# A second merge product on 32x32 tiles, wide state maps, halved sample state and merged transfers in an RWKV-7 + gMLP step

## The chip, the cores and the metric

The kernel runs on one core of a Trainium2 chip. The metric is the device time of one execution, in microseconds (us). The kernel before takes 1367.78 us, the median of three runs (1367.05 to 1368.15). A core has a matrix engine (PE, with its weight loads shown as PEld), a vector engine (DVE), an activation engine (ACT), a general engine (POOL) and SP, which here only issues transfers (DMAs). ACT's queue issues some transfers too.

## The reference, cut to what matters

Two layers run over a prompt of 512 tokens and a sample of 8 sequences of 4 tokens, with the same weights. Layer 0 is RWKV-7 time mixing, layer 1 a chunked gMLP; a final norm follows.

```python
proj = h @ w_in                      # r, k, v, two low-rank inputs, z
xm = sh + (prev - sh) * mu           # token shift
wf = w0 + tanh(wd) @ w2              # decay, low rank
decay = exp(-exp(-softplus(-wf) - 0.5))
a = sigmoid(a0 + ad @ a2)
kk = kk / max(sqrt(sum(kk * kk)), 1e-12)
def step(S, inp):                    # per head, S is 64 x 64
    sa = einsum('bhvk,bhk->bhv', S, -kk_t)
    S = (S * w_t[:, :, None, :]
         + sa[..., None] * (kk_t * a_t)[:, :, None, :]
         + v_t[..., None] * k_t[:, :, None, :])
    return S, einsum('bhvk,bhk->bhv', S, r_t)
o = (group_norm(y) + bonus) * silu(z)
out = o @ w_out
```

There are 32 heads of 64. The outputs are the final activations of prompt and sample, the shift rows and the final states of layer 0 for both, and the sample's normalised gate values of layer 1.

## The kernel before, in words

**Tiling.** The heads are taken in 16 pairs, p = 0 to 15: head "even" on partitions 0 to 63 and head "odd" on 64 to 127 of one 128-wide block. The prompt is cut into 8 chunks of 64 tokens. Inside a chunk the recurrence is turned into matrix products: `gram` makes the products of the chunk's scaled rows (G, one 64x128 block per chunk and head), `lanes` and `merge` invert a unit lower triangle per chunk from 16x16 blocks up (`lanes` does the 16x16 ones on DVE, `merge` joins them to 32 and 64 by products on PE), and `chain` carries the 64x64 state from chunk to chunk. `sample` does the same for the 8 short sequences at once.

**The 16x16 blocks change layout through memory.** `gram` writes G to a scratch tensor du (four transfers), SP reads the diagonal 16x16 blocks of it back as lu, one block per partition (L553, four transfers of 16 partitions each). n, the factors of the normalisation, go the same way (dn at L509, ln at L512, four each). `lanes` works on lu (L626 to L662) and leaves lz. SP writes lz to the diagonal blocks of a scratch tensor dz (L666, four), whose other blocks stay zero, and reads it back as Zf with tokens on partitions (L668). `merge` transposes Zf on DVE (L680, into T), forms a first product pm (L690), copies it (P, L692), forms the second product pm2 (L698), copies two of its blocks per 32 back into Zf (L702), and does the same once more at the next size (L712 to L728).

**`chain`.** L771 forms pz from the inverse and copies it as XA (L778). L791 and L792 multiply XA by the G block and by BKT, the transposed key rows, into the state maps pm; pn (L797) gives the offsets. MB, RS and ND are read out of them on DVE (L799 to L807). Then sb (L811) and RS (L812) alternate seven times, PE and DVE, once per step over the chunks; py, pfs and ps (L821 to L854) give outputs and final state.

**`sample`.** W, 128 rows, is spread by a mask over eight sequences into We (128x512, L891), one product pst with BT (L894) gives the state's change, two DVE operations add and scale it (L895, L896), and pso (L900) transposes the result out.

**What sets the order.** A projection's products come in units of three matmuls (L257, L258, L259: each operand is split into a high and a low part); 64 units, 16 each for r, k, v and z of a pair, make a period. Everything else hangs on the dict PLAN: at unit 64 p + u of the stream the next step of `gram`, `lanes`, `merge` and so on is emitted (`steps`, `on`, `play`). PE keeps that order exactly; DVE, ACT, POOL and SP are ordered by the scheduler, which follows the emission with priorities. BANKS says which part of PSUM each product uses.

**Start and end.** Before the periods the constants, x, the shift state and the first weights are loaded, x is normalised and transposed (pth, L219), and the low-rank inputs are projected. In the last period `out_stream` joins the fill: it loads xT (L1099), the outputs of layer 0 (ofl, L1090) and multiplies them by the output weights (po).

Of the kernel before, what the change touches and what calls it, by code (L numbers as in the profile page):

```python
# [29 lines left out]

BANKS = {'pbk0': 's', 'plw0': 'y', 'pak': 'g', 'pge1': 'wa', 'pgo0': 'y', 'pge0': 'g', 'pv': 'g', 'pxt': 's'}

def _consts():
# [16 lines left out]
    c["d0"] = np.broadcast_to(d0, (128, LW))  # L50
    c["maskb"] = b[:, None] == np.arange(8)[None, :]
    c["rowm"] = np.stack([ar == 0, ar == 1, b % 2 == 0, b % 2 == 1], 1)
# [15 lines left out]
def build(tc, A, O, off):  # L68
# [5 lines left out]
    with ctx:  # L74
# [7 lines left out]
        cst = cp.tile([128, A["consts"].shape[1]], F32, name="cst")  # L82
        Q.dma_start(cst, A["consts"])

# [22 lines left out]
        nhalf = cp.tile([128, 16], F32, name="nhalf")  # L107
        G.memset(nhalf, -0.5)


# [33 lines left out]
        with tc.tile_pool(name="st", bufs=1) as st:  # L144
# [11 lines left out]
            load_x(0)  # L156
            load_x(1)
            Q.dma_start(r0, rows(A["norm_g"]))
            load_x(2)
# [27 lines left out]
            def stats(h):  # L187

                n = 3 - h
                ms = st.tile([128, 3], F32, name=f"ms{h}")  # L190
                if h == 0:
                    G.memset(ms, 1.0)
                    S.activation(sqj[0:32], xs, AF.Square, scale=D**-0.5, accum_out=ms[0:32, 2:3])
                S.activation(sqj, xt[:, 2 * h, :], AF.Square, scale=D**-0.5, accum_out=ms[:, 0:1])
                bs0 = st.tile([128, 2, 6], F32, name=f"bs0{h}")
                mv0 = st.tile([128, 2], F32, name=f"mv0{h}")
                for j in range(2):
                    V.bn_stats(bs0[:, j, :], xt[:, 2 * h + 1, 512 * j : 512 * j + 512])
                V.bn_aggr(mv0, bs0)
                V.tensor_scalar(ms[:, 1:2], mv0[:, 0:1], mv0[:, 0:1], mv0[:, 1:2], op0=ALU.mult, op1=ALU.add)  # L200
                G.tensor_scalar(ms[:, 0:n], ms[:, 0:n], NORM_EPS, None, op0=ALU.add)
                G.tensor_tensor(out=ms[:, 0:n], in0=ms[:, 0:n], in1=nhalf[:, 0:n], op=ALU.pow)
                return ms
# [137 lines left out]

        du = [drm.tile([4, 2, 2, 64, 64], F32, name=f"du{i}") for i in range(2)]
        dz = [drm.tile([4, 2, 2, 64, 64], F32, name=f"dz{i}") for i in range(2)]
        zz = l0.tile([128, NCH, 64], F32, name="zz", tag="Zf", bufs=2)
        G.memset(zz, 0.0)
        for x in dz:
            Q.dma_start(x.rearrange("q h a s t -> (a s) (q h) t"), zz)
        cnt = [0]
# [146 lines left out]
        def norms(p, smp=None):  # L495
# [11 lines left out]
            dn = drm.tile([4, 2, 2, 64], F32, name=f"dn{p}", tag="dn", bufs=2)  # L507
            for g in range(4):
                Q.dma_start(dn[g], n2[32 * g : 32 * g + 2].rearrange("h (a t) -> h a t", t=64))  # L509
            ln = z["ln"] = l0.tile([64, 16], F32, name=f"ln{p}", tag="ln", bufs=2)  # L510
            for i in range(4):
                Q.dma_start(ln[16 * i : 16 * i + 16], dn.rearrange("q h a t -> (q h a) t")[:, 16 * i : 16 * i + 16])  # L512

# [16 lines left out]
        def gram(p):  # L530

            z = Z[p]
            AR, BK = z["AR"], z["BK"]
            GS = z["GS"] = [l0.tile([128, NCH, 128], F32, name=f"G{n}{p}", tag="G", bufs=4) for n in "EO"]
            for q in range(2):
# [11 lines left out]
            for h in range(2):  # L547
                for a, rs in enumerate(rw_):
                    Q.dma_start(d[:, h, a].rearrange("q s t -> s q t"), GS[h][rs, a::2, 0:64])
            lu = z["lu"] = l0.tile([64, 16, 16], F32, name=f"lu{p}", tag="lu", bufs=1)  # L550
            for i in range(4):
                b = slice(16 * i, 16 * i + 16)
                Q.dma_start(lu[b], d.rearrange("q h a s t -> (q h a) s t")[:, b, b])  # L553
            yield
# [37 lines left out]
        def turn(p):  # L592

            z = Z[p]
            AR, BK, GS, v = z["AR"], z["BK"], z["GS"], xv
            BKT = z["BKT"] = l0.tile([128, NCH, 128], F32, name=f"BKT{p}", tag="BKT", bufs=1)
            for q in range(2):
                ps = wh(f"pbk{q}")
                for j in range(4):
                    T.transpose(ps[:, 128 * j : 128 * j + 128], BK[:, 4 * q + j].rearrange("p a b -> p (a b)"), ident)  # L600
                S.activation(BKT[:, 4 * q : 4 * q + 4, :], c128(ps), AF.Copy)
                yield
# [16 lines left out]
        def lanes(p):  # L619
# [43 lines left out]
            d = dz[p % 2]  # L663
            for i in range(4):
                b = slice(16 * i, 16 * i + 16)
                Q.dma_start(d.rearrange("q h a s t -> (q h a) s t")[:, b, b], lz[b])  # L666
            Zf = z["Zf"] = l0.tile([128, NCH, 64], F32, name=f"Zf{p}", tag="Zf", bufs=2)
            Q.dma_start(Zf, d.rearrange("q h a s t -> (a s) (q h) t"))  # L668

        def merge(p):  # L670
# [25 lines left out]
            for c in range(NCH):  # L696
                for rs in (e_, o_):
                    T.matmul(ps[rs, 64 * c : 64 * c + 64], P1[rs, 64 * c : 64 * c + 64], Zf[rs, c, :], start=True, stop=True)  # L698
            pz = ps.rearrange("p (c j) -> p c j", j=64)
# [56 lines left out]
        def chain(p):  # L756

            z = Z[p]
            GS, AR, W, ZR, BKT, Dt = (z[n] for n in ("GS", "AR", "W", "ZR", "BKT", "D"))
            XA = l0.tile([128, NCH, 64], F32, name=f"XA{p}", tag="XN", bufs=1)  # L760
# [24 lines left out]
            for j in range(4):  # L785
                for h, hs in enumerate(rw_):
                    for a, rs in enumerate(rw_):
                        c = 2 * j + a
                        if c:
                            x = XA[rs, 2 * j + h, :]  # L790
                            T.matmul(pa[a][hs, 128 * j : 128 * j + 64], x, GS[h][rs, c, 64:128], start=True, stop=True)  # L791
                            T.matmul(pa[a][hs, 128 * j + 64 : 128 * j + 128], x, BKT[rs, c, 64 * h : 64 * h + 64], start=True, stop=True)  # L792

            pn = bank("pn", "s")
            for c in range(NCH):
                for h, hs in enumerate(rw_):
                    T.matmul(pn[hs, 64 * c : 64 * c + 64], BKT[:, c, 64 * h : 64 * h + 64], W[:, c, 64 * h : 64 * h + 64], start=True, stop=True)  # L797
            ND = l0.tile([128, NCH, 64], F32, name=f"ND{p}", tag="XN", bufs=1)
# [35 lines left out]
        def sample(p):  # L834
# [6 lines left out]
            def w5(name):  # L841
                return lt.tile([128, 512], F32, name=f"{name}{p}", tag="m", bufs=2)

# [44 lines left out]
            V.tensor_tensor(out=ysr, in0=ps[:, 0:64], in1=GR, op=ALU.add)  # L888
            We = w5("We")
# [4 lines left out]
            T.matmul(ps, BT, We, start=True, stop=True)  # L894
            V.tensor_tensor(out=s0, in0=ps, in1=s0, op=ALU.add)  # L895
            V.tensor_tensor(out=v8(s0), in0=v8(s0), in1=z["D"][:, 8:16, None].to_broadcast([128, 8, 64]), op=ALU.mult)  # L896
# [99 lines left out]
        def finish(i):  # L996
# [4 lines left out]
        PLAN = dict(  # L1001
            gram=(38, 42, 43),
            bonus=(53, 55),
            lanes=(53, 54, 55, 57, 59, 65, 66, 67, 67, 68, 68, 70, 70, 75, 75, 75),
            lora=(62, 65, 69, 71, 74),
            fold=(55, 66, 79, 87),
            smp0=78,
            merge=(88, 92, 100, 106),
            burst=96,
            flip=91,  # L1010
            chain=(107, 117, 121, 129, 132, 135, 137, 141, 142, 142),
            smp=(107, 109, 111, 116, 119, 124),
            tail=145,
            tail_end=(151, 160),
        )
        agenda = {}

        def on(p, u, f):
            agenda.setdefault(64 * p + u, []).append(f)

# [72 lines left out]
        def out_stream():  # L1093
# [3 lines left out]
            wts = halves(*raw.pop(0))  # L1097
            for m in range(0, KD, 2):
                OQ.dma_start(xT[:, m : m + 2], xfd[:, m : m + 2])  # L1099
# [367 lines left out]
```

## Time and profile before

| what | value |
|---|---|
| median of three runs | 1367.78 us (1367.05 to 1368.15) |
| the profiled execution's own time | 1372.8 us |
| its span, mean granted clock | 1371.0 us, 0.989 |
| PE busy | 1307.7 us (95%), 14764 records |
| DVE, ACT, POOL busy | 994.0 (73%), 683.4 (50%), 163.2 (12%) us |
| gMLP part (930 to 1371) | 441.0 us, PE 433.9 busy |

The span is shorter than the execution's time by 1.8 us that lie around it. A busy PE is not PE at its peak, and a wait counts only on the chain of work that ended last; an engine's idle time elsewhere costs nothing. In the rows, "pm" stands for several products of `merge` and `chain`, which the line tells apart.

### The profile page before, as it was taken

How to read it: one execution, taken by the hardware profiler on the slowest of the kernel's cores; microseconds unless marked ns; L12 is line 12 of the kernel's file. 1: busy time of each engine (PE TensorE's matmuls, PEld its weight loads, DVE VectorE, ACT ScalarE, POOL GpSimd, SP SyncE). 2: the span in 40 equal slices, each digit the busy share in tenths (PEclk: the TensorE clock that was granted, in tenths of full speed). 3: DMA queues.
4: the chain of work that ended last, by engine and by line, in shares of the span. 5: the costliest groups of instructions: out<-in, count | busy, mean ns of one | idle time of the engine just before them, and what ended most of it. 6: DMA issues, size and time to landing. Idle time of an engine off the chain costs nothing.

```text
span 1371.0 us, 36002 instructions
## 1 busy us (share of the span) xinstructions
PE 1307.7 (95%) x14764; PEld 1228.4 (90%) x14764; DVE 994.0 (73%) x2296; ACT 683.4 (50%) x1582; POOL 163.2 (12%) x352
## 2 busy tenths in 40 slices
PE   5879999999999999999999979999999999999998
PEld 4879889888988988898898868999999999999997
DVE  5668988988898897889889767555446755656566
ACT  5555666566556656655665634234333323223334
POOL 2310222122022112102211200000000000000000
PEclk9999999999999999999999989999999999999999
DMA  4423343333333334332332254523222323232411
GB/s 149 115 64 83 85 102 90 75 105 86 93 86 98 87 76 101 78 91 68 81 82 66 69 162 129 151 66 100 77 79 80 88 72 95 66 108 60 144 54 66
DMA packets 282759, 124.30 MB, mean 91 GB/s; under 512 B 117618, under 2 KB 275460, under 8 KB 282596
## 3 DMA queue, kind: packets, MB, share of 16 engines
q1 hardware_dynamic: 262948, 106.94, 29.7%
q10 hardware_dynamic: 19648, 15.08, 3.7%
q8 instruction: 116, 1.90, 0.6%
q14 instruction: 47, 0.39, 0.1%
HBM read 102.02 MB, written 19.95 MB: 89 GB/s over the span
## 4 chain that ended last, share of the span: by engine, by line
PE 53%; DVE 23%; issue 7%; DMA 6%; ACT 5%; POOL 3%; SPq 2%; DVEq 0%; ACTq 0%; POOLq 0%
POOL m L930 3%; PE gz_p L257 3%; PE gz_p L259 2%; PE gu_p L257 2%; PE gz_p L258 2%; PE gu_p L259 2%; PE gu_p L258 2%; PE gv_p L258 2%; PE gv_p L259 2%; PE gv_p L257 2%; PE v_p L257 2%; DMA lu<-du 2%; PE go__p L258 2%; PE go__p L257 2%; PE go__p L259 2%
## 5 line engine op out<-in xcount | busy, mean ns | idle before, releaser
L257 PE MATMUL v_p<-hh,v_h 128*128 128x272 f32 x256 | 84.8, 331 | 0.0
L257 PE MATMUL k_p<-hh,k_h 128*128 128x272 f32 x256 | 81.5, 318 | 0.0
L257 PE MATMUL r_p<-hh,r_h 128*128 128x272 f32 x256 | 79.2, 309 | 0.0
L257 PE MATMUL z_p<-hh,z_h 128*128 128x272 f32 x256 | 78.2, 305 | 0.0
L257 PE MATMUL gv_p<-hh,gv_h 128*128 128x272 f32 x256 | 75.6, 295 | 0.0
L257 PE MATMUL gz_p<-hh,gz_h 128*128 128x272 f32 x256 | 75.6, 295 | 0.0
L259 PE MATMUL k_p<-hh,k_l 128*128 128x272 f32 x256 | 74.4, 291 | 1.0 <-DVE k_l L127 1.0
L259 PE MATMUL z_p<-hh,z_l 128*128 128x272 f32 x256 | 74.4, 291 | 0.0
L258 PE MATMUL z_p<-hl,z_h 128*128 128x272 f32 x256 | 74.3, 290 | 0.0
L258 PE MATMUL gv_p<-hl,gv_h 128*128 128x272 f32 x256 | 74.3, 290 | 0.0
L259 PE MATMUL gv_p<-hh,gv_l 128*128 128x272 f32 x256 | 74.2, 290 | 0.0
L257 PE MATMUL gu_p<-hh,gu_h 128*128 128x272 f32 x256 | 74.2, 290 | 0.0
L259 PE MATMUL r_p<-hh,r_l 128*128 128x272 f32 x256 | 74.0, 289 | 0.0
L258 PE MATMUL k_p<-hl,k_h 128*128 128x272 f32 x256 | 74.0, 289 | 0.0
L259 PE MATMUL gu_p<-hh,gu_l 128*128 128x272 f32 x256 | 74.0, 289 | 0.0
L258 PE MATMUL gu_p<-hl,gu_h 128*128 128x272 f32 x256 | 74.0, 289 | 0.0
L259 PE MATMUL gz_p<-hh,gz_l 128*128 128x272 f32 x256 | 74.0, 289 | 0.0
L258 PE MATMUL v_p<-hl,v_h 128*128 128x272 f32 x256 | 74.0, 289 | 0.0
L259 PE MATMUL v_p<-hh,v_l 128*128 128x272 f32 x256 | 73.9, 289 | 0.0
L258 PE MATMUL r_p<-hl,r_h 128*128 128x272 f32 x256 | 73.8, 288 | 0.0
L258 PE MATMUL gz_p<-hl,gz_h 128*128 128x272 f32 x256 | 73.8, 288 | 0.0
L378 POOL COPY shl<-raw 128x9 f32<-128x9 f32 x49 | 20.7, 423 | 292.9 <-ACT raw L375 292.9
(453 smaller groups left out, 4928.7 us busy)
## 6 DMA issues: line engine op xcount, KB each, us to landing
k_r<-rw_in SPq DMA_DIRECT2D x16, 512.0 KB
r_r<-rw_in SPq DMA_DIRECT2D x16, 512.0 KB
v_r<-rw_in SPq DMA_DIRECT2D x16, 512.0 KB
z_r<-rw_in SPq DMA_DIRECT2D x16, 512.0 KB
gv_r<-gm_in SPq DMA_DIRECT2D x16, 512.0 KB
gu_r<-gm_in SPq DMA_DIRECT2D x16, 512.0 KB
gz_r<-gm_in SPq DMA_DIRECT2D x16, 512.0 KB
go_r<-gm_out SPq DMA_DIRECT2D x24, 256.0 KB
```

Source lines behind the costliest of these rows:

```text
L257: T.matmul(ps, whi, ahi, start=first, stop=False)
L258: T.matmul(ps, whi, alo, start=False, stop=False)
L259: T.matmul(ps, wlo, ahi, start=False, stop=last)
L378: G.tensor_copy(shl[:, :, f], raw[:, 512:553:5])
L930: G.tensor_tensor(out=m2, in0=m2, in1=nhalf[:, 0:9], op=ALU.pow)
```

## The change

1. **pm2** (second product of `merge`): of each 64x64 block only the two 32x32 blocks on the diagonal are read, so only those are computed, four 32x32 products a chunk in place of two 64x64.
2. **GK**: G and BKT come to lie side by side in one tile [128, 8, 2, 192], so that one product of 128 columns replaces two of 64 for the state maps. The tile has two buffers; before G had four half-size ones, BKT one.
3. **Sample state**: the mask is taken modulo four, We has 256 columns, and two products of 256 columns, one on each half of the rows, go to two banks; two DVE additions of half width follow.
4. **Transfers**: du and dz have 65 rows a block, so that the diagonal is one regular pattern: lu and dz are one transfer each in place of four, ln one in place of four, dn two in place of four, lr (low-rank weights) two in place of four with a repeated source and one buffer in place of two. Zf becomes two, the zeroing of dz four in place of two.
5. **Start**: the constants are loaded behind xs and the first two x loads, an activation on a column of ones stands early, one small addition moves from POOL to DVE.
6. **End**: the four xT loads are spread over the first output groups.
7. **PLAN and BANKS** have other numbers. `early` with late=0 changes nothing.

```diff
@@ second product of merge
             for c in range(NCH):
-                for rs in (e_, o_):
-                    T.matmul(ps[rs, 64 * c : 64 * c + 64], P1[rs, 64 * c : 64 * c + 64], Zf[rs, c, :], start=True, stop=True)
+                for b0 in range(4):
+                    rs, j0 = slice(32 * b0, 32 * b0 + 32), 32 * (b0 % 2)
+                    js = slice(64 * c + j0, 64 * c + j0 + 32)
+                    T.matmul(ps[rs, js], P1[rs, js], Zf[rs, c, j0 : j0 + 32], start=True, stop=True)
@@ wide operand
-            GS = z["GS"] = [l0.tile([128, NCH, 128], F32, name=f"G{n}{p}", tag="G", bufs=4) for n in "EO"]
+            GK = z["GK"] = l0.tile([128, NCH, 2, 192], F32, name=f"GK{p}", tag="G", bufs=2)
+            GS = z["GS"] = [GK[:, :, h, 0:128] for h in range(2)]
...
-                            T.matmul(pa[a][hs, 128 * j : 128 * j + 64], x, GS[h][rs, c, 64:128], start=True, stop=True)
-                            T.matmul(pa[a][hs, 128 * j + 64 : 128 * j + 128], x, BKT[rs, c, 64 * h : 64 * h + 64], start=True, stop=True)
+                            T.matmul(pa[a][hs, 128 * j : 128 * j + 128], x, GK[rs, c, h, 64:192], start=True, stop=True)
@@ sample state
-            mb = C("maskb")[:, :, None].to_broadcast([128, 8, 64])
-            V.tensor_tensor(out=v8(We), in0=W[:, None, :].to_broadcast([128, 8, 64]), in1=mb, op=ALU.mult)
+            We = s("We", 256)
+            mb = C("maskb")[:, :, None].to_broadcast([128, 4, 64])
+            V.tensor_tensor(out=We.rearrange("p (b v) -> p b v", v=64), in0=W[:, None, :].to_broadcast([128, 4, 64]), in1=mb, op=ALU.mult)
             yield
-            ps = wm("pst")
-            T.matmul(ps, BT, We, start=True, stop=True)
-            V.tensor_tensor(out=s0, in0=ps, in1=s0, op=ALU.add)
+            ps = wm("pst"), wh("psu")
+            for a, rs in enumerate(rw_):
+                T.matmul(ps[a][:, 0:256], BT[rs], We[rs], start=True, stop=True)
+            for a in range(2):
+                cs = slice(256 * a, 256 * a + 256)
+                V.tensor_tensor(out=s0[:, cs], in0=ps[a][:, 0:256], in1=s0[:, cs], op=ALU.add)
@@ transfers
+        def diag(d):
+            return bass.AP(d.tensor, d.offset, [[16 * 65, 64], [64, 16], [1, 16]])
+
+        def whole(d, a):
+            return d[:, :, a, 0:64].rearrange("q h s t -> s (q h) t")
...
-            for i in range(4):
-                b = slice(16 * i, 16 * i + 16)
-                Q.dma_start(lu[b], d.rearrange("q h a s t -> (q h a) s t")[:, b, b])
+            Q.dma_start(lu, diag(d))
...
-            for i in range(4):
-                b = slice(16 * i, 16 * i + 16)
-                Q.dma_start(d.rearrange("q h a s t -> (q h a) s t")[:, b, b], lz[b])
+            Q.dma_start(diag(d), lz)
...
-            Q.dma_start(Zf, d.rearrange("q h a s t -> (a s) (q h) t"))
+            for a, rs in enumerate(rw_):
+                Q.dma_start(Zf[rs], whole(d, a))
...
-            lr = lH.tile([128, 2, 128], F32, name=f"lr{p}", tag="lr", bufs=2)
-            for rs in (e_, o_):
-                Q.dma_start(lr[rs, 0, :], A["rw_w2"][0, :, pb])
-                Q.dma_start(lr[rs, 1, :], A["rw_a2"][0, :, pb])
+            lr = lH.tile([128, 2, 128], F32, name=f"lr{p}", tag="lr", bufs=1)
+            for i, n in enumerate(("rw_w2", "rw_a2")):
+                w = A[n][0, :, pb]
+                Q.dma_start(lr[:, i, :], bass.AP(w.tensor, w.offset, [[0, 2]] + [list(x) for x in w.ap]))
@@ the plan
-            gram=(38, 42, 43),
-            bonus=(53, 55),
-            lanes=(53, 54, 55, 57, 59, 65, 66, 67, 67, 68, 68, 70, 70, 75, 75, 75),
+            gram=(38, 43, 45),
+            bonus=(55, 59),
+            lanes=(46, 47, 48, 50, 51, 52, 53, 56, 58, 59, 60, 63, 63, 66, 70, 72),
...
-            merge=(88, 92, 100, 106),
+            merge=(88, 92, 98, 105),
...
-            chain=(107, 117, 121, 129, 132, 135, 137, 141, 142, 142),
-            smp=(107, 109, 111, 116, 119, 124),
-            tail=145,
-            tail_end=(151, 160),
+            chain=(107, 115, 120, 128, 131, 135, 137, 139, 141, 141),
+            smp=(106, 108, 112, 115, 115, 122),
+            tail=149,
+            tail_end=(157, 160),
@@ the output stream
-            for m in range(0, KD, 2):
-                OQ.dma_start(xT[:, m : m + 2], xfd[:, m : m + 2])
+            ldx = lambda m: OQ.dma_start(xT[:, m : m + 2], xfd[:, m : m + 2])
+            ldx(0)
             yield
...
+                if k0 == 0 and m in (0, 2, 4):
+                    ldx(m + 2)
```

**How the order moves.** The rows below are instructions in the order in which they stand on one engine (line, operation, result<-operands, shape; "xN" is N of a kind in a row; "rw_" ends are cut names of weights). First SP in a steady period, from the end of the lanes' data to its return as Zf; before:

```order
L906 DMA sample_wkv<-so_8308 64x4x64 x4
L851 DMA sn_8504<-state_wkv 64x4x64 x2
L666 DMA dz_309<-lz_8373 16x16x16 x4
L851 DMA sn_8504<-state_wkv 64x4x64
L120 DMA z_r<-rw_in 128x8x128
L668 DMA Zf_8379<-dz_309 128x8x64
L832 DMA prompt_wkv<-fs_8501 64x2x64
L424 DMA lr_11668<-rw_w 64x128
L425 DMA lr_11668<-rw_a 64x128
```

and after the change:

```order
L916 DMA sample_wkv<-so_8219 64x4x64 x4
L857 DMA sn_8408<-state_wkv 64x4x64 x3
L121 DMA z_r<-rw_in 128x8x128
L673 DMA dz_311<-lz_8201 64x16x16
L435 DMA lr_10759<-rw_w 128x1x128
L435 DMA lr_10759<-rw_a 128x1x128
L676 DMA Zf_8204<-dz_311 64x8x64 x2
L841 DMA prompt_wkv<-fs_8390 64x2x64
```

The load of z's weights now stands ahead of dz, and the two lr loads stand between dz and Zf; before they stood behind Zf.

Next DVE at the end of the lanes in a steady period (lM, ltm, lR and lz are the lanes', RS one step of the chain, r_l the low part of r's weights for the next pair, L the decay's running sum); before:

```order
L652 TENSOR_REDUCE lM_8238<-ltm_8237 64x64
L812 SCALAR_TENSOR_TENSOR RS_8168<-sb_8350,D_6754,ND_8216 128x64
L656 TENSOR_TENSOR ltm_8237<-lR_8239,lM_8238 64x512
L588 SCALAR_TENSOR_TENSOR zs_8143<-th_8340,zs_8143 128x272
L659 TENSOR_REDUCE lR_8239<-ltm_8237 64x8x8
L812 SCALAR_TENSOR_TENSOR RS_8168<-sb_8384,D_6754,ND_8216 128x64
L662 TENSOR_TENSOR lz_8373<-lR_8239,ln_7927 64x16x16
L127 TENSOR_TENSOR r_l<-r_r,r_h 128x1024
L812 SCALAR_TENSOR_TENSOR RS_8168<-sb_8408,D_6754,ND_8216 128x64
```

and after:

```order
L821 SCALAR_TENSOR_TENSOR RS_8936<-sb_9091,D_7571,ND_8970 128x64
L661 TENSOR_REDUCE lM_8891<-ltm_8890 64x64
L128 TENSOR_TENSOR r_l<-r_r,r_h 128x1024
L665 TENSOR_TENSOR ltm_8890<-lR_8892,lM_8891 64x512
L597 SCALAR_TENSOR_TENSOR zs_8920<-th_9087,zs_8920 128x272
L668 TENSOR_REDUCE lR_8892<-ltm_8890 64x8x8
L821 SCALAR_TENSOR_TENSOR RS_8936<-sb_9126,D_7571,ND_8970 128x64
L671 TENSOR_TENSOR lz_9041<-lR_8892,ln_8697 64x16x16
```

r_l stood behind lz and between two RS steps; it now stands in the lanes' last stretch, ahead of lz and of the second RS shown.

Last ACT near the end of the last full period (o_2_r are output weights, oh the high part of ofl, th and zs the gate); before:

```order
L120 DMA o_2_r<-rw_out 128x4x128
L1099 DMA xT<-xfd 128x1088 x4
L800 ACTIVATE RS_13200<-ND_13248 128x64
L601 ACTIVATE BKT_13288<-pbk_13289 128x512
L586 ACTIVATE th_13304<-z_p 128x272
L587 ACTIVATE zs_13177<-z_p 128x272
L1075 ACTIVATE oh_13163<-ofl_13358 128x544
L1075 ACTIVATE oh_13163<-ofl_13362 128x544
```

and after:

```order
L121 DMA o_2_r<-rw_out 128x4x128
L1112 DMA xT<-xfd 128x1088
L1089 ACTIVATE oh_13040<-ofl_13225 128x544
L1089 ACTIVATE oh_13040<-ofl_13229 128x544
L809 ACTIVATE RS_13071<-ND_13105 128x64
L1112 DMA xT<-xfd 128x1088 x2
L595 ACTIVATE th_13159<-z_p 128x272
L596 ACTIVATE zs_13057<-z_p 128x272
```

One xT load stands ahead of the RS step in place of four, and the two oh copies have moved ahead of it.

More of the change, by code (lines that the diff above doesn't have):

```diff
@@ L108, in build @@
         G.memset(nhalf, -0.5)
+        warm = cp.tile([128, 1], F32, name="warm")
+        S.activation(warm, ones[:, 0:1], AF.Square)
         hh = cp.tile([128, KD, 2, HT], F32R, name="hh")
@@ L157, in build @@
             load_x(1)
+            Q.dma_start(cst, A["consts"])
             Q.dma_start(r0, rows(A["norm_g"]))
@@ L758, in chain @@
             z = Z[p]
-            GS, AR, W, ZR, BKT, Dt = (z[n] for n in ("GS", "AR", "W", "ZR", "BKT", "D"))
+            GS, AR, W, ZR, GK, Dt = (z[n] for n in ("GS", "AR", "W", "ZR", "GK", "D"))
             XA = l0.tile([128, NCH, 64], F32, name=f"XA{p}", tag="XN", bufs=1)
@@ L796, in chain @@
                 for h, hs in enumerate(rw_):
-                    T.matmul(pn[hs, 64 * c : 64 * c + 64], BKT[:, c, 64 * h : 64 * h + 64], W[:, c, 64 * h : 64 * h + 64], start=True, stop=True)
+                    T.matmul(pn[hs, 64 * c : 64 * c + 64], GK[:, c, h, 128:192], W[:, c, 64 * h : 64 * h + 64], start=True, stop=True)
             ND = l0.tile([128, NCH, 64], F32, name=f"ND{p}", tag="XN", bufs=1)
```

43 lines of the change are left out of this document (21 added, 22 removed).

## The prediction, made before the changed kernel ran

> **What bounds the kernel now.** I read the busy shares first, then the same by stage, then PE's waits, then the chain of work that ended last. The page's first part and the table by stage (columns: stretch and its length, then busy time of PE, PEld, DVE, ACT, POOL, granted clock, DMA share, GB/s):
>
> ```profile
> PE 1307.7 (95%) x14764; PEld 1228.4 (90%) x14764; DVE 994.0 (73%) x2296; ACT 683.4 (50%) x1582; POOL 163.2 (12%) x352
> ...
> 0.00:17.00 17.00, 3.77 (x19) 3.31 (x19) 5.67 (x14) 7.57 (x13) 2.97 (x16) 1.00 0.78 252
> 17.00:131.60 114.60, 100.66 (x978) 92.72 (x977) 81.34 (x182) 66.18 (x157) 24.49 (x54) 0.94 0.32 77
> 131.60:755.90 624.30, 607.99 (x8506) 554.43 (x8505) 532.11 (x1322) 388.73 (x969) 116.15 (x247) 1.00 0.36 87
> 755.90:817.20 61.30, 50.99 (x646) 45.70 (x645) 44.00 (x109) 28.15 (x67) 6.79 (x13) 0.92 0.43 116
> ```
>
> PE is busy 95%, but the average hides four stages. In the first 17 us PE does almost nothing. From 131.6 to 755.9 run thirteen periods of 624.3 / 13 = 48.0 us, with PE busy 46.8 and DVE 40.9 of each. The period after them lasts 61.3. The rest, gMLP, is untouched. PE's waits (what waited, for what: total us, times, longest):
>
> ```profile
> PE png L182 <- DMA r<-norm_g: 9.6, 1, 9.6
> PE pm L690 <- DVE T L680: 7.6, 1, 7.6
> PE pys L950 <- DVE ZR L693: 5.8, 14, 0.6
> PE sb L811 <- DVE lR L644: 4.9, 1, 4.9
> PE pth L219 <- DVE xsh L210: 3.6, 1, 3.6
> PE sb L811 <- DVE RS L812: 2.9, 14, 0.2
> PE pyt L948 <- DVE yn L943: 1.4, 1, 1.4
> ```
>
> The long ones come once, at the start, in pair 0 and at the end. Those with 14 times are short, but each sits behind a chain of DVE work. The chain of waits through one steady period (start, duration, what; an "xN" is a block of N matmuls) says whether PE's own work counts there:
>
> ```profile
> 660.34 1.08 PE py L821 x32
> ...
> 673.88 0.61 DVE ZR L693
> ...
> 681.78 0.38 PE pm L723 x32
> ...
> 683.82 1.10 PE pz L771 x32
> ...
> 687.90 1.06 ACT k_h L126
> ...
> 703.34 0.51 DVE lz L662
> 703.85 1.05 DVE r_l L127
> ...
> 708.13 0.20 PE py L821
> ```
>
> From py to py is 47.79 us. The chain runs through DVE and ACT up to ZR (674.5), then on PE until the v projection ends, when k_h starts (687.9), then on DVE as far as r_l (704.9), then on PE. So only some 13 us from pys to the end of v, and 3 before py, are on PE; in the other 30 or so a shorter matmul only makes PE wait longer for DVE.
>
> **PE's shorter work, in the steady periods.** The second merge product's old price, and the old price of the pair of products that the wide operand replaces:
>
> ```profile
> 95.57 1.08 PE pm L698 x32
> ...
> 690.01 0.27 PE L791 MATMUL pm<-GE,XA 64*64 64x64 f32 x1
> ...
> 691.19 1.15 PE L797 MATMUL pn<-W,BKT 128*64 128x64 f32 x32
> ...
> 693.38 1.02 PE L894 MATMUL pst<-We,BT 128*128 128x512 f32 x2
> ...
> L894 PE MATMUL pst<-We,BT 128*128 128x512 f32 x32 | 16.3, 592 | 0.0
> ```
>
> pm2: 1.08 us for 32 records on 64x64 tiles. On 32x32 tiles it has 64 records; the 32 of L723, of the same shape, take 0.38, so 64 take 0.76 if records set the time, and 0.38 if the streamed columns do. I take 0.65, nearer the rows' own rate: -0.43. State maps: from 690.01 until pn starts at 691.19 is 1.18 us for 28 products of 64 columns, two records each. The wide form has 14 of 128 columns; L771, the same shape with 16, takes 1.10, so 14 take 0.96: -0.2. Sample state: two records span 1.02 with 0.59 each, so one starts 0.43 after the other, 0.86 in all. By row halves each streams half as many columns, and both run side by side on the two halves of the rows: 0.43 if nothing overlaps worse: -0.4. One stop of the projection stream fewer: -0.1. Together -1.1 us a period.
>
> Where they lie: pm2 stands between py and pys, in a stretch that ends with ZR on DVE, so its -0.43 is hidden; the cover is 14 us of DVE and ACT, and gone it would give the 0.43. The state maps and the sample state lie in the stretch from k_h to r_l: hidden too. DVE itself loses little: MB, RS, ND stay; the add into the state becomes two of half width; the We product halves (about -0.3). Against that the new places put r_l ahead of lz and between two RS steps: r_l takes 1.05, so one sb can wait up to 0.85 for its RS, and the new last place of pso (unit 58) can meet s up to 0.9 late; sb loses its 2.9 / 14 = 0.2 and the earlier places of lanes take work out of DVE's late rush. From -1.5 (all of PE's work plus some stalls) to +0.5 (the two new waits, half hidden). I take -0.35, near the hidden end: fourteen periods, **-5**.
>
> **Merged transfers.** Rows of the chain for a usual lu and for a period where it was held up, then the issue of dz and of Zf and the instruction that reads Zf:
>
> ```profile
> 305.46 1.81 DMA lu<-du
> ...
> 419.09 1.08 PE py L821 x32
> ...
> 449.74 3.78 DMA lu<-du
> ...
> 468.17 1.08 PE py L821 x32
> ...
> 656.09 1.78 SPq L666 DMA_DIRECT2D dz<-lz  x4
> ...
> 661.04 0.38 SPq L668 DMA_DIRECT2D Zf<-dz  x1
> ...
> 664.93 0.71 DVE L680 STREAM_TRANSPOSE T<-Zf 128x512 f32<-128x512 f32 x1 [0.15 <-DMA Zf<-dz]
> ```
>
> SP issues one of these four every 0.45 us (1.78 / 4), so a merged lu, ln or dz leaves SP 1.35 us sooner. In most periods the data arrives in time anyway: nothing. The period from 419.09 to 468.17, where lu took 3.78, lasted 49.1, and the mean of thirteen is 48.0 against 47.8 in the one shown: 0.2 x 13 = 2.6 us in all: **-2.5**, from 0 to -2.6. Zf is at its limit: the transposition waited 0.15 for it. dz one issue instead of four wins 1.35, r_l ahead of lz may lose 1.05: nothing, unless lr holds it (last rival).
>
> In pair 0 the same transfers stand on the chain alone, with PE waiting 7.6:
>
> ```profile
> 68.14 1.61 SPq L553
> 70.29 2.94 DMA lu<-du
> ...
> 84.80 1.75 DMA dz<-lz
> 86.69 3.73 DMA Zf<-dz
> ```
>
> lu, dz save 1.35 each in issue; ln and the earlier lanes add up to 2; the second Zf issue costs 0.4. **-3**, from -1 to -5.
>
> **Start.** The 702 KB of constants (sizes are from the list of DMA issues) go behind xs and the first two x loads. At the 252 GB/s of the first 17 us that is 2.8 us; x arrives that much sooner. The add on DVE instead of POOL, and an early table load, give tenths. PE's 9.6 + 3.6 us of waiting shrink by what x wins, if the weights are there: **-2.5**, from -1 to -3.5.
>
> **The last full period** lasts 61.3, 13.5 over the others. Its rows:
>
> ```profile
> 787.50 2.00 ACTq L1099 DMA_DIRECT2D xT<-xfd  x4
> ...
> 788.02 7.65 DMA lu<-du
> ...
> 797.20:802.00 4.80, 4.77 (x26) 4.80 (x27) 4.73 (x18) 0.60 (x1) 0.00 (x0) 0.64 0.02 3
> ```
>
> Four xT loads of 544 KB go out on ACT's queue just as lu does, and lu takes 7.65 instead of 1.8. DVE stands behind it, and sb waits the 4.9 of PE's waits above; then the granted clock is 0.64 for 4.8 us, which costs 4.8 x 0.36 = 1.7, and PE's later waits for out-projection loads follow. After the change one xT load is out before lu, two stand behind the step that writes RS, one later, and lu is one issue: its wait falls to 0 to 2. So -3 to -5 of the stall, -1 to -2 of clock, and 0 to -6 of later waits if they move up too: **-8**, from -3 to -13. The last pyt waited 1.4 for yn. Its place is six units later, that of the step which feeds it four; a unit is 47.8 / 64 = 0.75 us on the mean, so two units cover nearly all of it, less where units run closer together: **-1**, from -0.7 to -1.4.
>
> Sum: -2.5 - 3 - 5 - 2.5 - 8 - 1 = -22. The profiled execution took 1372.8 (span 1371.0), 5.0 above the median of the runs, 1367.78. 1372.8 - 22 - 5.0 = 1345.8, or **1346 us**.
>
> **Rivals.**
> *PE's work counts everywhere.* If the new places make DVE's chains as short as PE's work, a period wins 1.1 and another 0.4 of the short stalls: 14 x 1.5 = 21 in place of 5: 1330. For it: PE 46.8 of 48.0 busy. Against: the chain above.
>
> *Only the ends move.* The steady periods stay (0), the slow ones too (their late ln and lu have another cause, as the same sn and weight loads remain), and the end gives 4: -2.5 - 3 - 4 - 1 = -10.5: 1357.
>
> *Other side: lr holds Zf.* The merged lr loads, 64 KB each, read a source that begins with a two-fold repeat, and now stand on SP between dz and Zf. If such a load is cut along that repeat, 131 KB go over two of the sixteen DMA engines. In the last period's flood the queues moved 258 GB/s at a share of 0.83:
>
> ```profile
> 788.00:797.20 9.20, 4.37 (x52) 3.55 (x48) 3.32 (x11) 2.63 (x6) 0.00 (x0) 1.00 0.83 258
> ```
>
> 258 / (16 x 0.83) = 19.4 GB/s an engine, so 66 KB an engine take 3.4 us, from two issues of 0.45 after dz's. Zf waits dz's 1.75 anyway, so its last pieces come up to 3.4 + 0.9 - 1.75 = 2.5 late, with a slack of 0.3 to 1.35 (dz's single issue, less r_l or not). It decides from the point where this exceeds the slack. At 2 us net: 14 x 2 = 28 lost, pair 0's gain down to 1: -2.5 - 1 + 28 - 2.5 - 8 - 1 = +13: 1381. Against: before, four lr loads stood behind Zf and no row shows how a load is cut. The Trainium skill's page "DMA: Bandwidth & Descriptors", section "Rules for kernel authors", says that an outermost dimension smaller than 16, such as a leading zero-stride broadcast of c copies, confines the whole DMA to at most c engines. By that rule the two engines are certain, and only Zf's slack is open; no run here shows it yet.
>
> **How the numbers follow.** Forecast 0.46, PE everywhere 0.2, only the ends 0.2, lr 0.12, the change not doing what it says (waits I have not seen eat it) 0.02. Range: down to just beyond 1330, up past 1357 and the weak form of the lr case (0.9 us a period, 14 x 1.25 = 17.5 over the forecast): **1326 to 1364**; the bounds of the terms alone (taken together about half as far as their sum) give 1333 to 1358. A difference of 0.2% is about what a measurement of this kernel can tell. Faster by more: 0.46 + 0.2 + 0.2 less 0.02 = 0.84; within 0.2%: 0.04; slower: 0.12.
>
> **What would show it.** pm2 near 0.65, the wide maps near 0.96 and pst near 0.43 start to start, with the py to py distance down by under 0.7 and pys still waiting for ZR; the wait on T for pair 0 down from 7.6 to about 5; lu's last landing under 4 us and no clock of 0.64 at the end; pth some 2.5 earlier. It is wrong if a steady period is over 48.0 or under 46.8, if T waits for Zf in each period, or if the last full period still lasts over 58.

## The result, and the profile after

The changed kernel takes 1388.13 us (median of four runs, 1383.06 to 1389.95), the kernel before 1367.97 (four runs, 1367.05 to 1369.05): a ratio of 1.0141, 95% interval 1.0112 to 1.0170. It is slower by some 20 us where 22 less were forecast. The profiled execution took 1383.06 us (span 1381.3, clock 0.992); the other three runs were 4 to 7 us longer, at clocks of 0.984 to 0.987. So the two profiles that are compared below lie 10.3 us apart (1371.0 and 1381.3), the medians 20; the rows can place the 10, and no profile shows where the rest lies.

The busy times of the page, and the table by stage of the changed kernel (stretch, its length, busy PE, PEld, DVE, ACT, POOL, clock, DMA share, GB/s):

```profile
PE 1297.6 (94%) x14860; PEld 1215.8 (88%) x14860; DVE 987.7 (72%) x2314; ACT 687.2 (50%) x1583; POOL 152.2 (11%) x350
...
129.90:771.10 641.20, 602.15 (x8584) 546.57 (x8583) 527.22 (x1335) 391.81 (x970) 108.77 (x247) 1.00 0.33 85
771.10:827.20 56.10, 48.23 (x652) 43.64 (x653) 43.54 (x110) 28.00 (x68) 7.06 (x13) 0.94 0.40 110
```

PE is busy 10 us less, as the shorter products should make it, and DVE 6 us less. Yet the thirteen steady periods take 641.2 in place of 624.3: 16.9 more. The first py comes 1.7 earlier than before (129.9 for 131.6), the last full period is 5.2 shorter, and what follows is nearly the same. So between the two profiles the loss has one place, the steady periods.

PE's waits of the changed kernel (what waited, for what: total, times, longest), then DVE's waits for transfers:

```profile
PE pm L708 <- ACT P L700: 12.8, 11, 1.4
PE pys L960 <- DVE YN L954: 12.1, 14, 1.2
...
PE pso L910 <- DVE s L906: 7.8, 14, 1.3
PE pla L445 <- ACT xw L450: 7.0, 16, 0.8
PE pm L698 <- DVE T L688: 6.5, 1, 6.5
...
PE pth L221 <- DVE xsh L212: 1.8, 1, 1.8
```

```profile
DVE T L688 <- DMA Zf<-dz: 24.6, 13, 2.3
DVE lu L635 <- DMA lu<-du: 13.4, 16, 2.9
```

The same two of the kernel before:

```profile
DVE lu L626 <- DMA lu<-du: 6.4, 3, 5.8
DVE T L680 <- DMA Zf<-dz: 0.8, 3, 0.5
```

Two waits have grown at the head of DVE's chains. T, the transposition of Zf, waited for it in three periods of before; now it waits 24.6 us in 13 times, of which 22.0 in the eleven steady periods that load lr, 2.0 each. lu is waited for in every period. One period of the chain of waits, and SP's issues and the transposition in it (the bracket gives the idle time before an instruction and what ended it):

```profile
327.77 1.08 PE py L830 x32
...
343.47 0.33 PE pys L960
...
356.48 1.07 ACT k_h L127
...
377.13 1.08 PE py L830 x32
```

```profile
324.56 0.60 SPq L673 DMA_DIRECT2D dz<-lz  x1
326.88 0.57 SPq L435 DMA_DIRECT2D lr<-rw_w  x1
327.50 0.54 SPq L435 DMA_DIRECT2D lr<-rw_a  x1
328.13 1.81 SPq L676 DMA_DIRECT2D Zf<-dz  x2
...
334.26 0.71 DVE L688 STREAM_TRANSPOSE T<-Zf 128x512 f32<-128x512 f32 x1 [2.05 <-DMA Zf<-dz]
```

From py to pys it is 15.7 us; before it was 674.53 - 660.34 = 14.2. The two stretches behind pys, to k_h and on to the next py, take 33.7 together where they took 33.6, so the 1.5 us come from T. Between dz and Zf stand the two lr loads, as the last rival of the prediction had them. In the periods after the last lr load (the two before 771) py to pys is 14.35 again and T does not wait.

### The profile page after: what moved, and what is told of

Same layout as the page of the kernel before. It is cut to its first block, busy times and chain, and to the rows that moved or that the text cites. A ratio compares the mean times of both kernels' runs of the same rounds, so it can differ in the third digit from the quotient of the medians.

```text
span 1381.3 us, 35899 instructions
## 1 busy us (share of the span) xinstructions
PE 1297.6 (94%) x14860; PEld 1215.8 (88%) x14860; DVE 987.7 (72%) x2314; ACT 687.2 (50%) x1583; POOL 152.2 (11%) x350
## 4 chain that ended last, share of the span: by engine, by line
PE 66%; DVE 11%; DMA 8%; ACT 6%; issue 4%; POOL 3%; SPq 1%; POOLq 0%; ACTq 0%; DVEq 0%
DMA lu<-du 5%; PE v_p L259 3%; POOL m L940 3%; PE gz_p L259 3%; PE gz_p L261 2%; PE gz_p L260 2%; PE gu_p L259 2%; PE gu_p L260 2%; PE gu_p L261 2%; PE gv_p L260 2%; PE gv_p L261 2%; PE gv_p L259 2%; PE pgo L553 2%; PE po L259 2%; PE po L260 2%
## 5 line engine op out<-in xcount | busy, mean ns | idle before, releaser
L259 PEld LDWEIGHTS v_p<-hh,v_h 128*128 128x128 f32 x256 | 48.1, 188 | 8.3 <-issue 3.2
```

What stands on the lines that cost most here:

```text
L259: T.matmul(ps, whi, ahi, start=first, stop=False)
```

## The experiments

Three readings of these rows competed. **E (engines)**: the lr loads, whose source begins with a two-fold repeat, run on few of the DMA engines and hold Zf's pieces there. **Q (queue)**: SP itself stands at lr, which waits for its only buffer, and issues twice before Zf. **W (waits)**: lr is innocent, and the new places made the period longer.

### lr behind Zf

```diff
+            if p >= 4:
+                G.tensor_tensor(out=warm[0:1, 0:1], in0=lr[0:1, 0, 0:1], in1=Z[p - 3]["Zf"][0:1, 0, 0:1], op=ALU.add)
             xa = hd(f"xa{p}")
```

The added reader holds lr's buffer until Zf has landed, so the next load can't go out earlier.

> The changed kernel, but each pair of lr loads must wait for a one-element POOL operation that reads lr's last user data and Zf, so on SP they stand behind Zf. Theory Q (queue: SP stands at lr between dz and Zf, waits there for lrl on DVE and issues twice, so Zf leaves late) and theory E (engines: the lr bytes on two DMA engines hold Zf's pieces): T no longer waits (under 0.2 us in place of 2.0), the ten periods of 49.2 to 50.5 fall to 47.7 to 48.1, the time falls by 14 to 18, to about 1371. Theory W (waits that the new places brought by themselves, at pso, sb, P): T's wait goes but the period stays above 49 and the time above 1384.

Measured: 1373.47 us against 1367.44 of the kernel before, ratio 1.0048 (1.0029 to 1.0066), in seven runs. DVE's waits and a period of the chain:

```profile
DVE lu L637 <- DMA lu<-du: 14.5, 16, 2.9
...
DVE T L690 <- DMA Zf<-dz: 5.9, 4, 3.8
```

```profile
328.01 1.08 PE py L832 x32
...
342.30 0.33 PE pys L962
...
376.57 1.08 PE py L832 x32
```

T's wait goes from 24.6 to 5.9, of which 3.8 once in the last period; py to pys is 14.3 and the periods 47.9 to 48.7 (and one of 50.1), somewhat longer than E and Q had them. The ratio falls by 0.9%, some 13 us where 14 to 18 were expected. W as the main cause is out; E and Q both remain.

### lr in four loads, in front of Zf

```diff
-            for i, n in enumerate(("rw_w2", "rw_a2")):
-                w = A[n][0, :, pb]
-                Q.dma_start(lr[:, i, :], bass.AP(w.tensor, w.offset, [[0, 2]] + [list(x) for x in w.ap]))
+            for rs in (e_, o_):
+                Q.dma_start(lr[rs, 0, :], A["rw_w2"][0, :, pb])
+                Q.dma_start(lr[rs, 1, :], A["rw_a2"][0, :, pb])
```

> The changed kernel with four lr loads of 32 KB, each from a source without a repeat, in place of two of 64 KB; one buffer; three of the four stand ahead of Zf on SP. Q: one more issue of 0.6 us ahead of Zf, so T's wait grows from 2.0 to about 2.5 and the period from 49.3 to about 49.9. E: the bytes now go over sixteen engines, so only the late issue is left: T's wait falls to 1.3 or less, the period to 48.7 or less.

Measured: 1373.08 us in its one run, periods 47.9 to 48.9 (and one of 54.0). Three loads stand ahead of Zf and its issue is 0.6 later, yet py to pys is 14.5. But DVE's order had moved too: there T stands behind the next pair's k, 7.3 us after py in place of 4.4, so Zf could be late for nothing. This run is no verdict between E and Q.

### The same order, the load's source turned

```diff
-                Q.dma_start(lr[:, i, :], bass.AP(w.tensor, w.offset, [[0, 2]] + [list(x) for x in w.ap]))
+                Q.dma_start(lr[:, i, :], bass.AP(w.tensor, w.offset, [list(w.ap[0]), [0, 2], list(w.ap[1])]))
```

Every instruction stays in its place; only the outermost dimension of the source is 64 rows in place of the repeat of two.

> The changed kernel with every engine's order as it is; only the source of each lr load repeats every row twice in a row (64 rows outermost) in place of the whole block twice (2 outermost). So the low-rank weights reach other partitions than they should and the values are not the reference's; sizes, places, waits and issues stay. Theory E (lr's bytes on two DMA engines hold Zf's pieces): T's wait falls from 2.0 to under 1.0, py to pys from 15.7 to 14.4 to 14.8, the period to 48.0 to 48.5, the time to 1370 to 1376. Theory Q (SP stands and issues between dz and Zf): the wait stays at 1.8 to 2.1, the period at 49.3, the time at 1383 to 1390. Half and half: a wait near 1.0 with a period near 48.6.

Measured: 1373.54 us, ratio to the kernel before 1.0033 (1.0015 to 1.0052), against 1.0141 for the change. DVE's waits and a period:

```profile
DVE lu L635 <- DMA lu<-du: 14.8, 16, 3.2
DVE T L688 <- DMA Zf<-dz: 6.5, 9, 1.6
```

```profile
323.75 1.08 PE py L830 x32
...
338.04 0.33 PE pys L960
...
371.87 1.08 PE py L830 x32
```

Zf is issued at the same time after py as in the changed kernel in most periods (0.4 to 0.6 there, 0.5 to 0.7 here), and T's wait falls, from 22.0 to 6.5 in the eleven periods with lr. That is E: the way the load is cut costs 1.4 us a period (22.0 - 6.5 over 11), and SP's standing (Q) no more than the 0.6 that is left. The packets in the traces agree. The two lr loads of a period are 256 packets of 512 bytes. In the changed kernel at most four of them are under way at once in each of the eleven periods, and the last ends 5.1 to 5.8 us after the first issue; here 10 to 13 are, and the last ends after 2.9 to 3.8. The Trainium skill's page "DMA: Bandwidth & Descriptors", section "Rules for kernel authors", says that a leading zero-stride broadcast of c copies confines a DMA to at most c engines; this pair of runs agrees: with c = 2 in each of two loads at most four packets are under way, and 1.1% of the kernel's time lies between a 2 and a 64 outermost.

### Merged lr on the kernel before

lr as in the change, the rest as before; on SP it stays behind Zf.

> The kernel before with lr merged as in the change (two loads of 64 KB with a repeat outermost, one buffer); on SP they stay behind Zf. E and Q both: T's wait stays under 0.3 on the mean, periods near 47.8, time 1366 to 1370. If merging itself costs wherever the loads stand (W): periods over 48.5.

Measured: 1371.58 us in its one run, periods 47.8 to 48.9, DVE waits 2.6 us for Zf in four times. Within the spread of the kernel before (1363.80 to 1373.92 in that session), so this one run shows no cost of merging where nothing urgent follows in the queue. There too, in most periods, at most four of lr's packets are under way at once.

### The old places

```diff
-BANKS = {'pbk0': 'sm', 'plw0': 'sm', 'pak': 'wa', ...
+BANKS = {'pbk0': 's', 'plw0': 'y', 'pak': 'g', ...
...
-            gram=(38, 43, 45),
-            bonus=(55, 59),
+            gram=(38, 42, 43),
+            bonus=(53, 55),
...
```

> The changed kernel with the numbers of PLAN and BANKS from before; products, wide operand, sample state and merged transfers stay. On SP lr stands behind Zf again, on DVE r_l behind lz. Q and E: T waits under 0.3, periods 47.3 to 47.8, time 1355 to 1366. W: also near 47.8, since the places are the old ones; it differs from Q in the run with lr behind Zf. If the PE work counts anywhere, the period is under 47.4.

Measured: 1430.27 us, ratio 1.0465 (1.0430 to 1.0501); a miss of every theory. T hardly waits, but:

```profile
PE pys L960 <- DVE ZR L701: 32.7, 14, 2.4
PE pbo L585 <- DVE bv L587: 22.5, 15, 1.6
```

The periods last 51.7 to 54.1. With the old places ZR and bv come late on DVE. The trace also shows a granted clock of 0.5 for 3.4 us thirteen times within these periods, where the changed kernel has none; at half speed that is, by an estimate, up to 13 x 3.4 x 0.5 = 22 of the 62 us that the thirteen periods lose against before. So in this combination the new parts do better with the new numbers. Which of the parts loses under the old ones was not separated.

### pm2 alone, and pm2 with the halved sample state, on the kernel before

```diff
-                for rs in (e_, o_):
-                    T.matmul(ps[rs, 64 * c : 64 * c + 64], P1[rs, 64 * c : 64 * c + 64], Zf[rs, c, :], start=True, stop=True)
+                for b0 in range(4):
+                    rs, j0 = slice(32 * b0, 32 * b0 + 32), 32 * (b0 % 2)
+                    js = slice(64 * c + j0, 64 * c + j0 + 32)
+                    T.matmul(ps[rs, js], P1[rs, js], Zf[rs, c, j0 : j0 + 32], start=True, stop=True)
```

> The kernel before with only the 32x32 tiles in pm2; DVE, ACT, SP and POOL keep their order. If pm2's 0.4 us are hidden behind DVE up to pys: py to pys 14.27 as before, period 47.8, time within 1 us of before. If PE's work counts: py to pys 13.9, period 47.4, time 5 to 6 less.

The second run has the sample state's edit as well.

> The kernel before with only the 32x32 tiles in pm2 and the halved sample state (about 0.4 + 0.4 us of PE work less per period). If they are hidden behind DVE's chains, as the prediction had it: periods 47.7 to 47.9, time 1366 to 1369. If PE's work sets the period: 47.0, time 1355 to 1358.

Measured for pm2 alone: 1364.88 us, ratio 0.9971 (0.9952 to 0.9990). The products and pys in one period, of the kernel before and then of this one:

```profile
670.83 1.15 PE L698 MATMUL pm<-Zf,P 64*64 64x64 f32 x32 [0.55 <-ACT P L692]
...
674.53 0.33 PE L950 MATMUL pys<-cst,YN 128*128 128x128 f32 x1 [0.41 <-DVE ZR L693]
```

```profile
671.35 0.75 PE L700 MATMUL pm<-Zf,P 32*32 32x32 f32 x64 [0.57 <-ACT P L692]
...
675.05 0.33 PE L952 MATMUL pys<-cst,YN 128*128 128x128 f32 x1 [0.80 <-DVE ZR L693]
```

pm2 spans 0.75 in place of 1.15, and pys waits 0.80 for ZR in place of 0.41: the 0.40 saved is the wait gained. The thirteen periods take 624.3 and 624.4 in these two profiles (626.3 in a second one of the kernel before). So the 0.3% that the timed runs gain is not seen there; of pm2's uses only those in pair 0 and after the periods have no such cover, by an estimate at most 3 x 0.4 = 1.2 us, so the rest of the 3 us is open.

Both edits together: 1371.31 us, ratio 1.0026 (1.0004 to 1.0048), periods near 48.0 with some up to 50.6. The new addition of the sample's part stands on DVE between the two bv operations, and pbo now waited 14.1 us for bv. Shorter PE work gained nothing and a moved order lost a little.

### Start and end alone, and with pm2

```diff
-        Q.dma_start(cst, A["consts"])
+        warm = cp.tile([128, 1], F32, name="warm")
+        S.activation(warm, ones[:, 0:1], AF.Square)
...
             load_x(1)
+            Q.dma_start(cst, A["consts"])
...
-            for m in range(0, KD, 2):
-                OQ.dma_start(xT[:, m : m + 2], xfd[:, m : m + 2])
+            ldx = lambda m: OQ.dma_start(xT[:, m : m + 2], xfd[:, m : m + 2])
+            ldx(0)
```

> The kernel before with only the change's start (constants behind xs and the first two x, early table load, the addition on DVE) and the spread xT loads. By the measured parts of the changed kernel: start 1.5 to 2.5 less, last full period 3 to 6 less (61.3 to 55 to 58), steady periods 47.8, time 1359 to 1364, faster than both kernels. If the last period's gain came from lu being one transfer: 59 to 61 there, time 1365.

> The kernel before with the 32x32 tiles in pm2, the change's start and the spread xT loads; DVE, ACT, SP and POOL ordered as in the run with start and xT alone. If the small gain of pm2 alone (ratio 0.997) is real and the ends give nothing: ratio 0.995 to 0.999, 1363 to 1367. If both ends gain with the shorter pm2: 1358 to 1362. Steady periods 47.8 either way.

Measured: 1368.77 us for the ends alone, ratio 1.0000 (0.9980 to 1.0019); 1365.60 with pm2, ratio 0.9978 (0.9965 to 0.9991). In the first of them pth starts 2.7 us earlier than in the first profile of before, but the first py only 0.1 (131.4 for 131.6), for pgo now waits longer (before: 2.2 of its 3.1 there):

```profile
PE pgo L544 <- DVE AS L524: 4.5, 2, 3.6
```

So an earlier x moves the wait to the next link of pair 0. With pm2 the first py was 4.4 earlier in one profile. But one profile says little here: the changed kernel and the run with lr behind Zf, whose edit acts from pair 4 on, have their first py at 129.9 and 134.9. The granted clock goes with that difference. In the stretch from 17.5 to 31.2 it is 0.50 with lr behind Zf and 1.00 in the changed kernel, and PE gets through 54 products in place of 74:

```profile
17.50:31.20 13.70, 13.37 (x54) 10.84 (x54) 6.60 (x15) 5.74 (x12) 0.71 (x1) 0.50 0.18 49
```

```profile
17.50:31.20 13.70, 13.28 (x74) 10.89 (x75) 9.52 (x24) 7.39 (x16) 2.22 (x7) 1.00 0.18 50
```

pm2 with the ends is 0.2% faster than the kernel before, pm2 alone 0.3%.

### The kernel before, profiled once more

> The kernel before, unchanged, profiled once more. If the 4.9 us wait of sb for the lanes in the last full period belongs to the kernel: that period lasts 60 to 62 again and lu lands after 7 to 8 us. If it was one execution's: 54 to 58, lu under 5, and the profiled time lies 3 to 6 nearer to the median than the first profile's 1372.8.

Measured: 1370.13 us. Its last full period is 815.78 - 757.95 = 57.8 in place of 61.3. The landing of lu in it (start, duration), and PE's wait at sb there:

```profile
789.60 4.79 DMA lu<-du
```

```profile
PE sb L811 <- ACT oh L1075: 1.5, 1, 1.5
```

lu took 4.8 in place of 7.65, and sb waited 1.5, for ACT, in place of 4.9. With pm2 alone, with all four xT loads still sent together, the period was even 54.8. So the long wait in the first profile was one execution's.

### Why 48 and not 47: lu

With lr out of the way the periods stay at 48, and DVE waits for lu in each. Theory **L** is that the late lu is what is left over 47.8, theory **D** that the wait only stands where other DVE work would. Three runs on top of the one with lr behind Zf: lu read in 1 KB pieces, lu in four transfers, and the same with gram at its old units so that lu stands ahead of the 512 KB load v_r.

```diff
-            Q.dma_start(lu, diag(d))
+            Q.dma_start(lu, bass.AP(d.tensor, d.offset, [[16 * 65, 64], [16, 16], [1, 16]]))
```

> The changed kernel with lr behind Zf, and lu read as one 1 KB piece per partition in place of sixteen of 64 bytes each, so that the lanes get wrong blocks and their values are not the reference's; one transfer as before, DVE's order around the lanes as it is. There lu lands 4.1 us after its issue and DVE waits for it in each period, 14.5 us in all. Theory L (the merged lu, late on the chain, is what is left over 47.8): landing about 2 to 2.5, DVE's wait under 3, periods 47.3 to 47.8, time 1364 to 1368. Theory D (the wait only takes the place of other DVE work): the wait goes, the periods stay at 47.9 to 48.5, time 1371 to 1375.

```diff
-            Q.dma_start(lu, diag(d))
+            for i in range(4):
+                Q.dma_start(lu[16 * i : 16 * i + 16], bass.AP(d.tensor, d.offset + 256 * 65 * i, [[16 * 65, 16], [64, 16], [1, 16]]))
```

> The changed kernel with lr behind Zf and lu as four transfers of 16 partitions again. From the first of four issues to the landing the kernel before takes 3.6 to 3.8, the one merged transfer 4.1. L: lu 0.3 to 0.5 earlier, periods 0.2 to 0.4 shorter, about 1368 to 1371. D: no change, 1372 to 1375. DVE's order there puts lu a few instructions later, so its wait falls under either.

The third has the four loads and these places:

```diff
-            gram=(38, 43, 45),
+            gram=(38, 42, 43),
```

> The changed kernel with lr behind Zf, lu in four again and gram at its old units 38, 42, 43; on SP lu then stands ahead of the 512 KB load v_r, as in the kernel before, where in all other versions of the change v_r is ahead of it. Theory V (v_r's bytes ahead of lu in the queue make it land late): from the last lu issue to the landing under 2.5 us in place of 4.1, lu no longer waited for. Theory M (merging alone made it late): refuted already by lu_four if its landing stays late there; then nothing changes here. For the time: if DVE's chain sets the period, 47.8 to 48.1 and 1367 to 1371; if the wait for lu did, under 47.6 and 1362 to 1365.

Measured: 1367.67 us, ratio 0.9998 (0.9977 to 1.0020); 1369.24, ratio 1.0004 (0.9983 to 1.0025); 1368.91, ratio 1.0008 (0.9994 to 1.0022). The 3.6 to 3.8 that the second expectation gives for lu in the kernel before are, in the prediction's row of 449.74, counted from the last of the four issues, not the first. In large pieces lu still lands late:

```profile
DVE lu L637 <- DMA lu<-du: 10.0, 15, 1.7
```

```profile
549.19 4.86 DMA lu<-du
...
741.74 4.05 DMA lu<-du
```

So small pieces aren't what makes it late: that part of L is refuted, and merging as such isn't shown to be the cause. With lu in four, DVE's order puts its use 1.5 us later and only one wait is left; the periods are 48.02 to 48.05, all but one of them. With lu ahead of v_r they are 48.26 to 48.30, all but one. There the last of lu's packets ends 1.4 to 2.6 after lu's last issue, with v_r ahead of the four 1.5 to 3.6; that fits v_r's bytes ahead of it but doesn't prove it. Two periods of that run:

```profile
570.74 1.08 PE py L833 x32
...
619.00 1.08 PE py L833 x32
...
667.27 1.08 PE py L833 x32
```

Whether lu is waited for or not, the usual period is 48.0 to 48.3, which fits D: the lateness of lu does not set it. The times say otherwise, and that stays open. All three runs lie some 0.4% below the one with lr behind Zf (1.0048), whose interval theirs do not meet, and the first two fell where L had them. In the profiles that gain is not in the periods: the thirteen take 627.9 us with lr behind Zf and 629.1, 628.4 and 629.7 in these three.

In each version with the new places one period, the one from about 520 to 570, lasts 50 to 54 (before 48.8 and 49.1). The traces show part of the reason. In four of the seven the granted clock is 0.5 there for 3.4 or 6.8 us from about 533 on, and these are the periods of 52 to 54; in the changed kernel and the runs with lr behind Zf and with lu ahead of v_r there is no such fall, and it lasts 50.1 to 50.4. With the load's source turned:

```profile
535.00:540.00 5.00, 5.00 (x52) 4.43 (x53) 3.99 (x9) 2.79 (x10) 1.11 (x3) 0.50 0.16 57
```

## Why the prediction was wrong

- **The step that failed** is the end of "Merged transfers": "nothing, unless lr holds it". It was priced at 0 and its rival at a chance of 0.12; the runs show 1.5 us in each of the eleven steady periods with lr, some 16.5 of the 16.9 between the profiles. The rival's place, mechanism and condition were right: lr stands between dz and Zf, its packets go at most four at a time, and it costs once Zf's slack is used up. The prediction's own sign of being wrong came, T waiting for Zf in each of these periods. The row that was at hand, Zf already waited for by 0.15, should have weighed more: a load put in front of a transfer without slack is a cost until something shows otherwise.
- **The rival's own time**, 1381, came nearer 1388 in part by luck. It had 28 us for lr (2 us over 14 periods), where 16.9 are measured, and some 15 of gains, where the profiles have 1.7 up to the first py and 5.2 in the last full period.
- **Steady periods, PE's work, -5**: the sizes were about right (pm2 spans 0.75 with its last product's 0.19 in it, against 0.65; the wide maps 1.02 from start to the next block against 0.96; the sample's two products 428 ns each, side by side) and so was their being hidden: pm2's 0.40 turned up as pys's wait. But the gain of 0.35 a period had no row of its own, and no run shows it: with lr behind Zf the thirteen periods take 627.9 us, before 624.3 and 626.3.

```profile
357.86 1.09 PE L801 MATMUL pm<-GK,XA 64*64 64x128 f32 x28
358.88 1.15 PE L806 MATMUL pn<-W,GK 128*64 128x64 f32 x32
...
L902 PE MATMUL pst<-We,BT 64*128 64x256 f32 x32 | 11.1, 428 | 0.0
```

- **New waits**: pso at its new place waits 7.8 in 14 times, 0.56 each, but up to 1.3 where 0.9 was the bound. sb's waits for RS fell from 2.9 to 0.7, once, as the small gain there had it; the new wait of up to 0.85 did not come as a rule. pla's 7.0 for xw was not named, and pys, forecast to wait for ZR still, waits for YN.
- **The last period, -8**, was mis-sized because it stood on one execution. The second profile of before has 57.8 there, the change 56.1. lu's last landing, forecast under 4, took 6.0 in the changed kernel, and the granted clock still falls there (0.71 from 810 to 815). In its bounds, -3 - 1 + 0 makes -4 and not -3. The same 5 us were counted twice: once as a stall to be won, and again when the profiled 1372.8 was brought down to the median by 5.0. The last pyt's wait fell from 1.4 to 0.4, as its -1 had it.
- **Start -2.5 and pair 0 -3**: pth came 2.3 earlier and lz of pair 0 three earlier, but the first py only 1.7, and between executions that number moves by more (129.9 and 134.9 above). PE's wait on T there is 6.5, not about 5. Zf, now in two, took longer there (3.73 before), and pla and pso had new waits. The changed kernel's chain in pair 0:

```profile
80.22 2.47 DMA dz<-lz
82.71 0.62 SPq L676
83.79 4.74 DMA Zf<-dz
```

- **The slow periods, -2.5**: not won. lu got later, not earlier. In a usual period of before its four issues took 1.8 and it landed 3.2 after the first; merged it lands 3.1 to 5.1 after its one issue in the steady periods. And du starts 3.5 later after py (27.2 for 23.8, the medians of the periods), 2.2 of which stay with lr behind Zf; with gram at its old units, in the last run above, 0.8 are left.

## What to carry to other kernels

Before merging transfers or moving one, list what stands behind it on its queue and ask which of those has no slack; a load whose source begins with a two-fold repeat showed no cost at the end of the queue (one run of the kernel before with lr merged, within that kernel's spread) and cost 1.1% in front of a transfer that an engine on the chain of waits was already waiting for. Where the chain of waits runs through another engine, a shorter product only lengthens the wait behind it; read that wait before and after, as with pys (0.41 to 0.80). And take a one-off stall as won only if a second execution has it too.

## What the runs showed of the hardware that was not expected

- The outermost dimension of a load's source, 2 or 64, with all else in place, changed the landing of the next transfer on the same queue: T's waits fell from 24.6 us in 13 times to 6.5 in 9, 1.4 a period. At most four of the two loads' packets were under way at once with a 2, 10 to 13 with a 64.
- Reading 1 KB pieces in place of 64-byte ones did not bring lu in sooner: 3.7 to 4.9 us from issue to landing in the chain's rows between 549 and 747, where the run with lr behind Zf, which differs in the pieces alone, has 3.9 to 4.5.
- Executions of one kernel differ by up to 12 us (1363.42 to 1375.72 for the kernel before in one session); between two profiles of it the last full period alone varied by 3.5.
- Where the granted clock fell to 0.5 differs from profile to profile: in the first 100 us it was at 0.5 for 10.2 us in the changed kernel and for 30.7 with lr behind Zf, and the first py came 5 later.
